# Attention scores on all 128 rows of the array, by padding with zeros, in a two-layer diffusion transformer step

## The chip, the cores and the metric

One core of a Trainium2 chip. The time is device microseconds (us) of one execution of the whole program. Before the change three runs gave 918.04, 919.28 and 920.19 us; the median is 919.28.

## The reference

One inference step of a hybrid backbone with two layers of width 1024. There are 128 prompt (context) tokens and 256 sample (latent) tokens that share all weights, and 128 cached keys and values. Each layer has a mixer (differential attention, a short gated convolution, a chunk MLP, all from one input projection and into one output projection) and a squared-ReLU MLP of hidden width 4096. What matters here is the attention, with 4 heads; a head's queries and keys have two components of 64 features each:

```
s = einsum('bqhcd,bkhcd->bchqk', q, k) * 64 ** -0.5    # c: the two components
p = softmax(s, axis=-1)
a = p[:, 0] - lam * p[:, 1]
o = einsum('bhqk,bkhd->bqhd', a, v)
```

Prompt queries read the 128 prompt keys. Sample queries read the 128 cached keys and the 256 sample keys (384 columns). Sample queries and keys take an axial rotation first (rotary positions). The result must be near fp32.

## The kernel before

Activations lie with features on partitions and tokens along the free dimension: `x` is 128 x 8 x 384. Weights stream from HBM in chunks of 128 x 1024 fp32 values. ScalarE rounds each chunk to a high part (`whi`, line 201), VectorE subtracts to get the low part (`wlo`, line 203), and TensorE multiplies three times per contraction step: high by high, high by low, low by high (lines 220 to 222). These long products fill nearly all of TensorE's time.

All engines run in an order written out at build time. `tick()` counts the contraction steps of the long products, and every side task is a generator that yields how many steps may pass before its next stage; the table `WAIT` holds these numbers. So the score products, transposes and value products stand at fixed places between the long products in TensorE's queue, and each of the other engines has its own fixed order too. Two further kinds of work are woven in: modulation products on TensorE (`pm`, line 262, which use 32 columns of the array) and modulation sums on VectorE (line 314).

Per head:

- `keys(h)` (line 653): the cached keys are loaded, the sample's keys are rotated (`rope_apply`: one shuffle on VectorE, three products and sums on GpSimd), and the sample's and cached keys are split. The high part `kh` holds each component on both halves of the partitions (lines 666 and 669). The low part `kl` holds component 0 on rows 0 to 63 and component 1 on rows 64 to 127 (line 670).
- `queries(h)` (line 672): the sample's queries are rotated and split into `qs`, per component a tile whose own half holds the high part (line 682) and whose other half holds the low part (line 685). With `kh` on both halves, one 128-row product gives high by high plus low by high.
- `attention(h, u)`: `u` = 0 is the prompt's block of queries, 1 and 2 are the sample's two blocks. The prompt's scores are plain fp32 products of 64 rows (line 728; an fp32 product shows as two instructions in the trace). The sample's are one 128-row product (line 731) and one 64-row product with the low key part (line 732), for each of the two components. Behind the scores come the maximum (VectorE, line 736), exponentials (ScalarE, 741), the combination of the two softmaxes (747 and 749), the transposes (TensorE, 753), their copies (ScalarE, 762 and 764), the value products (TensorE, 776), the head's norm and its transposes (797).

The first `NPRE` heads of a layer (3 and 2) have their products ahead of the norm. Their shift by the bias is added later, in `first_heads`, by ScalarE instructions over the prompt's and the sample's columns (lines 698 and 703). The other heads (1 and 2) come in `later_heads`; ScalarE drains their queries from PSUM in a single instruction over 384 columns (line 715). The shift itself needs small products of its own in layer 0 (lines 463 and 471, with a copy on ScalarE between them, line 467).

Of the kernel before, what the change touches and what calls it, by code (L numbers as in the profile page):

```python
# [9 lines left out]
F32 = mybir.dt.float32  # L10
F32R = mybir.dt.float32r
# [4 lines left out]
P = 128  # L16
# [3 lines left out]
TP = 128  # L20
TS = 256
T = TP + TS
# [5 lines left out]
# heads of a layer whose products go ahead of the norm  # L28
NPRE = (3, 2)
# parts of the first modulation vector  # L30
PARTS = 4

# contraction steps between the stages of the work beside the long products, by layer
# [53 lines left out]
# columns of the packed small operands: those of all layers that come first, then the rest  # L87
# [5 lines left out]
# order of the 128-column tiles of the input projection  # L93
Q0, K0, V0, GB0, GC0, XI0, U0, VS0 = 0, 512, 1024, 1536, 1792, 2048, 2304, 2560

# tokens, followed by one column for the shift of each group
# [4 lines left out]
def dit_kernel(ctx, tc, xT, cT, wmod, wmodT, wall, ck, cv, ws, lam, bs_in, small, rope, ident_in, yT, kT_out, v_out):  # L101
# [10 lines left out]
    # ---- constants and inputs  # L112
# [16 lines left out]
    # silu of the two conditioning vectors, as padded stationary columns  # L129
# [8 lines left out]
    # ---- the order of work: every engine runs in the order below. What is not part of the long  # L138
    # products is cut into stages; a stage names how many contraction steps of the long products
    # go by before the next one.  # L140
# [33 lines left out]
    def steps(gen, n, every):  # L174
        """n stages of a generator"""
        for i in range(n):
            next(gen, None)
            if i < n - 1:
                yield every

    # ---- weight streaming
# [8 lines left out]
    def refill(r=None):  # L190
        """the next chunk of the weights, in two parts"""
        i = state["chunk"]
        if i == wall.shape[0]:
            return
        state["chunk"] = i + 1
        if r is None:
            r = raw_chunk(wall[i])
        hi = wpool.tile([P, 1024], F32R, tag="whi", name="whi", bufs=4)
        lo = wpool.tile([P, 1024], F32R, tag="wlo", name="wlo", bufs=4)
        ready.append((hi, lo))  # L200
        nc.scalar.copy(hi, r)  # L201
        yield 2
        nc.vector.tensor_sub(lo, r, hi.bitcast(F32))  # L203
# [13 lines left out]
    def mm3(out, w, a, wsl, asl, first, last):  # L217
        """out += w.T @ a from the parts of both, w stationary"""
        (wh, wl), (ah, al) = w, a
        mm(out, wh[wsl], ah[asl], start=first, stop=False)  # L220
        mm(out, wh[wsl], al[asl], start=False, stop=False)  # L221
        mm(out, wl[wsl], ah[asl], start=False, stop=last)  # L222

    # ---- modulation vectors, features on partitions: modv[d][:, v, dt, group]
# [4 lines left out]
    def mod_done(d, v, base, dts=slice(0, KT)):  # L229
        """modv[d][:, v] = base + b_mod, and what scales the normed input"""  # L230

        def column(o):
            c = sm[:, d * S_LAYER + o + dts.start : d * S_LAYER + o + dts.stop]
            return c.unsqueeze(2).to_broadcast([P, dts.stop - dts.start, 2])

        nc.vector.tensor_add(modv[d][:, v, dts], base[:, dts], column(S_BMOD + v * KT))
        if v in (1, 4):
            nc.vector.scalar_tensor_tensor(
                (amix if v == 1 else amlp)[d][:, dts],
                modv[d][:, v, dts],  # L240
                1.0,
                column(S_NMIX if v == 1 else S_NMLP),
                ALU.add,
                ALU.mult,
            )

    def mod_products():
        """on the tensor engine: one feature tile of the contraction per step"""
        for i, (d, v) in enumerate(MOD_PE):
            pm = ps.tile([P, 256], F32, tag="mod", name="pm", bufs=1)  # L250
            tr = work.tile([P, KT, 32], F32, name="tr", tag="rtmp", bufs=1)
            # the first vector comes in parts of its features
            n = per = PARTS if i == 0 else 1
            width = 256 // n
            for f in range(n):
                own = slice(f * width, f * width + width)
                for q in range(KT // per):
                    w = ahead if (i, f, q) == (0, 0, 0) else raw_chunk(wmod[i, f * KT // per + q])
                    for k in range(per):
                        kt = q * per + k  # L260
                        for j in range(4):
                            mm(  # L262
                                pm[32 * j : 32 * j + 32, own],
                                sct[:, kt, :],
                                w[:, (4 * k + j) * width : (4 * k + j + 1) * width],
                                start=(kt == 0),
                                stop=(kt == KT - 1),
                            )
                    yield
                dts = slice(f * KT // n, (f + 1) * KT // n)  # L270
                nc.vector.transpose(tr[:, dts].rearrange("p a b -> p (a b)"), pm[:, own])
                mod_done(d, v, tr[:, :, 0:2], dts)
                yield
# [4 lines left out]
    # the two silu vectors along the free dimension, on every partition  # L278
# [4 lines left out]
    def spread_silu():  # L283
        """their high and low parts as rows, 32 features of each tile a row; then the sums of both parts"""
# [21 lines left out]
    def mod_sums():  # L306
        """on the vector engine: one group of one tile of the vector's features per step"""
# [16 lines left out]
    # ---- RMS statistics over the features (partitions)  # L324
# [13 lines left out]
    def rsqrt_refined(y, a, ms):  # L338
        """y ~ ms^-0.5 made exact by one Newton step"""
# [15 lines left out]
    def normed(scale, shift, every):  # L355
        """the normed and modulated input, a feature tile per stage"""
# [23 lines left out]
    def scaled_high(dt, scale):  # L380
        """a feature tile without its tokens' norms, which products take on afterwards"""
# [24 lines left out]
    def finish_x(dt, pacc, gate, scale, last=False):  # L406
        """the residual stream's tile after a product, and what the next norm needs of it"""
# [12 lines left out]
    def proj_tiles(a, n=1, cols=T, name="acc", order=tuple(range(KT)), later=0, make=acc_tile):  # L420
        """128-column tiles of a weight, transposed: [column, token]"""
# [11 lines left out]
    def proj_tokens(a, width):  # L433
        """`width` columns of a weight, tokens on partitions: three tiles [token, column]"""
# [21 lines left out]
    def shift_products(raws, bias, t0, t1):  # L456
        """what the shift adds to the columns of the raw tiles: [column, tile, group]"""
# [17 lines left out]
    # padded conv input: 0 | prompt | 0 | sample | 0  # L475
# [3 lines left out]
    KSEG = ((0, 0, TP, 0), (1, TP, T, 2 * TP))  # L479

# [3 lines left out]
    def lambdas(d):  # L484
# [10 lines left out]
        # -(e1 - e2 + li)  # L495
# [5 lines left out]
    for d in range(DEPTH):  # L501
# [5 lines left out]
        def evict(i):  # L507
            """a head's keys or queries but for the shift's part, which comes later"""
# [20 lines left out]
        # ------------------------------------------------ mixer  # L529
        # products with the tiles of two heads go ahead of the norm  # L530
# [122 lines left out]
        def keys(h):  # L653
            """positions, and the parts of the keys by component: the high ones on both halves, the low
            ones next to the queries' high ones"""
# [7 lines left out]
            kl = work.tile([P, T], F32R, name="kl")  # L663
# [4 lines left out]
            for c, (own, other) in enumerate(((LO, HI), (HI, LO))):  # L668
                nc.scalar.copy(kh[other, c], k[own, TP:])
                nc.vector.tensor_sub(kl[own], k[own, TP:], kh[own, c].bitcast(F32))  # L670

        def queries(h):
            """positions, and the parts of the sample's queries by component: high and low ones on the
            two halves, the high ones on the component's own"""
# [12 lines left out]
        def first_heads():  # L687
            for h in range(NPRE[d]):
# [12 lines left out]
                for g, s0, s1, off in KSEG:  # L701
                    qq = q_t[:, h, s0:s1]
                    nc.scalar.activation(qq, qq, AF.Identity, bias=bias[:, 2 * h + 1, g : g + 1])
# [4 lines left out]
        def later_heads():  # L708
            for h in range(NPRE[d], NH):
# [5 lines left out]
                nc.scalar.mul(q_t[:, h % 3], pq[:, 0:T], 0.125)  # L715
# [4 lines left out]
        def attention(h, u):  # L720
            """softmaxes of 128 queries of a head, combined and applied to the values"""
# [3 lines left out]
            for c in range(2):  # L725
                r = slice(64 * c, 64 * c + 64)
                if u == 0:
                    mm(sc[c][:, 0:TP], q_t[r, h % 3, 0:TP], k_t[r, h % 3, 0:TP], start=True, stop=True)
                else:
                    cols = slice((u - 1) * P, u * P)  # L730
                    mm(sc[c][:, 0:T], qs[:, c, cols], kh[:, c], start=True, stop=False)
                    mm(sc[c][:, 0:T], qs[r, c, cols], kl[r], start=False, stop=True)  # L732
# [45 lines left out]
            # norm of the head's output, tokens on partitions  # L778
# [45 lines left out]
        def conv(ct):  # L824
            """short convolution, channels on partitions"""
# [65 lines left out]
        # output projection  # L891
# [7 lines left out]
        # ------------------------------------------------ MLP  # L899
        if d == 1:  # L900
            start(steps(sums, 2 * KT, wt["sums_up"]), 2)
        for f in range(2):
# [33 lines left out]
            def down(pt, w, c, cols):  # L936
                """half of the contraction of a tile"""
# [13 lines left out]
    # ---- the last tiles, a group of tokens after the other, and the final norm of each group  # L951
# [40 lines left out]
# the vectors (layer, which) in the order of their use, by the engine that makes them  # L992
# [6 lines left out]
def _tiles(w, cols):  # L999
    """[1024, cols of one 128-tile] -> [128, 8 * 128]"""  # L1000
# [5 lines left out]
def _pack(inp):  # L1006
# [6 lines left out]
    # [d, k, (v dt j c)] -> [v, kt, p, (j dt c)] and [v, dt, p, k]  # L1013
    # the first vector: [part, some kt, p, (kt j dt c)]
# [52 lines left out]
    # axial rotary tables by shape: partition = (component, axis, half, frequency)  # L1067
# [34 lines left out]
```

## Time and profile before

| | |
|---|---|
| span of the profiled execution, first to last instruction | 916.9 us |
| its device time apart from the span | not listed; the three runs' median is 919.28 us |
| TensorE products busy | 894.1 us, 98% |
| TensorE weight loads busy (they lie beside products) | 839.8 us, 92% |
| VectorE / ScalarE / GpSimd busy | 652.9 / 478.5 / 81.3 us |
| mean granted TensorE clock | 0.993 |
| data transfers | all issued by SyncE; queue kinds "hardware_dynamic" and "instruction" |

Times are microseconds from the span's start unless marked ns. A row of the timeline gives the start, the duration, the engine, the line, the operation, what it writes and reads, the shape, and in brackets the idle time before it and what ended that. Products are pipelined, so a product's duration (0.34 us) is longer than the distance between the starts of two of them (0.17 us); what a product costs TensorE's order is read from the starts. `64*128` is the part of the array that a product uses, rows by columns. The attention of layer 0 lies between 60 and 180 us, that of layer 1 between 500 and 600 us.

### The profile page before, as it was taken

To read this page: it belongs to the slowest core of one execution; us is meant where nothing else is said; L and a number is where in the kernel's file an instruction comes from. 1 tells how busy PE (TensorE), PEld (TensorE's weight loads), DVE (VectorE), ACT (ScalarE), POOL (GpSimd) and SP (SyncE) were. 2 spreads that over 40 slices of the span, in tenths; PEclk is the share of its full clock that TensorE was granted. 3 is DMA by queue.
4 is the path that set the end of the run, shared out by engine and by line. 5 is a ranking of instruction groups with operands and counts; after the bars stand their busy time and mean duration, and the time that the engine had idled before them with its cause. 6 is when DMAs were issued, how large, how long until landed. Compare 5 with 4: busy or idle time off the path is not lost.

```text
span 916.9 us, 14490 instructions
## 1 busy us (share of the span) xinstructions
PE 894.1 (98%) x5476; PEld 839.8 (92%) x5476; DVE 652.9 (71%) x1214; ACT 478.5 (52%) x938; POOL 81.3 (9%) x79
## 2 busy tenths in 40 slices
PE   5999999999999999999999999999999999999996
PEld 4766787999999999999998788999999999999996
DVE  4688886789888877879979877458886344555333
ACT  4557765446762226663336786534676223665331
POOL 0004320011000000000112340003000000000021
PEclk9999999999999999999999899999999999999998
DMA  9877566455656765566773323224465434333302
GB/s 346 298 274 252 192 209 226 165 182 161 209 188 226 227 214 180 183 198 226 221 234 101 125 76 95 91 93 138 163 221 169 137 117 136 115 133 121 115 1 69
DMA packets 48470, 156.55 MB, mean 171 GB/s; under 512 B 5392, under 2 KB 11024, under 8 KB 48400
## 3 DMA queue, kind: packets, MB, share of 16 engines
q1 hardware_dynamic: 48400, 155.63, 51.4%
q8 instruction: 43, 0.70, 0.3%
q14 instruction: 27, 0.22, 0.1%
HBM read 152.98 MB, written 2.62 MB: 170 GB/s over the span
## 4 chain that ended last, share of the span: by engine, by line
PE 91%; DVE 5%; DMA 1%; issue 1%; ACT 1%; POOL 1%; SPq 0%; DVEq 0%; ACTq 0%
PE pdn L220 10%; PE pdn L222 10%; PE pdn L221 10%; PE pup L221 9%; PE pup L220 9%; PE pup L222 9%; PE po L220 2%; PE po L221 2%; PE po L222 2%; PE pm L262 2%; PE pkq L220 2%; PE pkq L221 2%; PE pkq L222 1%; PE po L776 1%; PE nat L448 1%; PE sc L732 1%
## 5 line engine op out<-in xcount | busy, mean ns | idle before, releaser
L201 ACT CAST whi<-raw 128x1024 fp32r<-128x1024 f32 x182 | 190.0, 1050 | 293.3 <-PE pdn L221 150.9
L203 DVE TENSOR_TENSOR wlo<-raw,whi 128x1024 fp32r<-128x1024 f32 x182 | 224.6, 1240 | 64.9 <-ACT whi L201 64.8
L220 PE MATMUL pdn<-ah,whi 128*128 128x384 f32 (+2 forms) x528 | 174.7, 331 | 0.0
L221 PE MATMUL pdn<-al,whi 128*128 128x384 f32 (+2 forms) x528 | 174.6, 331 | 0.0
L222 PE MATMUL pdn<-ah,wlo 128*128 128x384 f32 (+2 forms) x528 | 174.6, 331 | 0.0
L220 PE MATMUL pup<-hh,whi 128*128 128x386 f32 x512 | 174.1, 340 | 0.0
L221 PE MATMUL pup<-hl,whi 128*128 128x386 f32 x512 | 173.6, 339 | 0.3
L222 PE MATMUL pup<-hh,wlo 128*128 128x386 f32 x512 | 172.8, 337 | 0.0
L314 DVE SCALAR_TENSOR_TENSOR junk<-raw,cb 128x1024 bf16<-128x1024 f32 x112 | 136.7, 1220 | 0.4
L221 PEld LDWEIGHTS pdn<-al,whi 128*128 128x128 f32 x528 | 99.2, 188 | 0.0
L220 PEld LDWEIGHTS pdn<-ah,whi 128*128 128x128 f32 x528 | 99.2, 188 | 0.0
L222 PEld LDWEIGHTS pdn<-ah,wlo 128*128 128x128 f32 x528 | 99.2, 188 | 0.0
L221 PEld LDWEIGHTS pup<-hl,whi 128*128 128x128 f32 x512 | 96.9, 189 | 1.1 <-DVE hl L387 0.9
L220 PEld LDWEIGHTS pup<-hh,whi 128*128 128x128 f32 x512 | 96.4, 188 | 0.3
L222 PEld LDWEIGHTS pup<-hh,wlo 128*128 128x128 f32 x512 | 96.5, 188 | 0.0
L336 POOL TENSOR_TENSOR sacc<-sacc,sq 128x384 f32<-128x384 f32 x23 | 29.4, 1279 | 675.6 <-ACT sq L329 533.7
L917 ACT ACTIVATE relu<-relu,ub 128x128 f32<-128x128 f32 (+1 forms) x128 | 51.1, 446 | 17.4 <-DVE relu L914 17.4
L398 DVE SCALAR_TENSOR_TENSOR x<-pdn,modv,x 128x128 f32<-128x128 f32 (+1 forms) x62 | 23.0, 413 | 43.9 <-PE pdn L222 43.9
L921 DVE TENSOR_TENSOR al<-relu,ah 128x384 fp32r<-128x384 f32 x64 | 35.6, 556 | 15.0 <-ACT ah L919 14.8
L220 PE MATMUL po<-y,whi 128*128 128x384 f32 x128 | 43.0, 336 | 0.0
L222 PE MATMUL po<-y,wlo 128*128 128x384 f32 x128 | 42.8, 334 | 0.0
L221 PE MATMUL po<-y,whi 128*128 128x384 f32 x128 | 42.8, 334 | 0.0
(198 smaller groups left out, 1414.1 us busy)
## 6 DMA issues: line engine op xcount, KB each, us to landing
raw<-in_wall_dram SPq DMA_DIRECT2D x182, 512.0 KB, 3.6
raw<-in_wmodT_dram SPq DMA_DIRECT2D x56, 512.0 KB, 4.3
raw<-in_wmod_dram SPq DMA_DIRECT2D x40, 512.0 KB, 5.7
raws<-in_wall_dram SPq DMA_DIRECT2D x6, 512.0 KB, 8.0
x<-in_xT_dram SPq DMA_DIRECT2D x8, 192.0 KB, 7.8
out_dram<-x SPq DMA_DIRECT2D x4, 256.0 KB, 2.6
mix<-in_cv_dram SPq DMA_DIRECT2D x2, 256.0 KB, 5.7
mix<-in_ws_dram SPq DMA_DIRECT2D x2, 256.0 KB, 6.0
```

The costliest lines, as they stand in the source:

```text
L201: nc.scalar.copy(hi, r)
L203: nc.vector.tensor_sub(lo, r, hi.bitcast(F32))
L220: mm(out, wh[wsl], ah[asl], start=first, stop=False)
L221: mm(out, wh[wsl], al[asl], start=False, stop=False)
L222: mm(out, wl[wsl], ah[asl], start=False, stop=last)
L262: mm(pm[32 * j : 32 * j + 32, own], sct[:, kt, :], w[:, (4 * k + j) * width : (4 * k + j + 1) * width], start=(kt == 0), stop=(kt == KT - 1),)
L314: nc.vector.scalar_tensor_tensor(junk, w, 1.0, cb[:, g], ALU.mult, ALU.mult, accum_out=mr[:, dt, g : g + 1])
L336: eng.tensor_add(stat["acc"], stat["acc"], sq)
L398: nc.vector.scalar_tensor_tensor(x[:, dt, a:b], pacc[:, a:b], gate[:, dt, g : g + 1], x[:, dt, a:b], ALU.mult, ALU.add)
L448: mm(o, ah, wh[:, cols], start=(kt == 0 and tt % n == 0), stop=False)
L917: nc.scalar.activation(r[:, s0:s1], r[:, s0:s1], AF.Relu, bias=ub[:, g : g + 1])
L921: nc.vector.tensor_sub(al[:, i], r, ah[:, i].bitcast(F32))
```

## The change

The low part of the keys becomes two static tiles per component, of 128 rows, with zeros in the other component's rows: component 0's low keys on rows 0 to 63 of `kl[:, 0]`, component 1's on rows 64 to 127 of `kl[:, 1]`. They meet all 128 rows of `qs`; the rows with the queries' low parts meet zeros. The prompt's queries go into tiles `qp`, again one per component with zeros in the other's rows, and meet all 128 rows of the prompt's keys. The zeros are written once, by GpSimd at the start; the rest of the program writes only the other halves. ScalarE therefore writes the prompt's queries in two 64-row instructions and the sample's in another one. To make room in SBUF, the program is built with a smaller DMA scratch. Comments are removed as well, which the diff below leaves out.

```diff
+    kl_t = [const.tile([P, 2, T], F32R, name=f"kl{i}") for i in range(2)]
+    qp_t = [const.tile([P, 2, TP], F32, name=f"qp{i}") for i in range(3)]
+    for t in (*kl_t, *qp_t):
+        nc.gpsimd.memset(t.bitcast(F32), 0.0)
...
         def keys(h):
...
-            kl = work.tile([P, T], F32R, name="kl")
+            kl = kl_t[h % 2]
...
-                nc.vector.tensor_sub(kl[own], k[own, TP:], kh[own, c].bitcast(F32))
+                nc.vector.tensor_sub(kl[own, c], k[own, TP:], kh[own, c].bitcast(F32))
...
         def first_heads():
...
-                for g, s0, s1, off in KSEG:
-                    qq = q_t[:, h, s0:s1]
-                    nc.scalar.activation(qq, qq, AF.Identity, bias=bias[:, 2 * h + 1, g : g + 1])
+                qb = bias[:, 2 * h + 1]
+                for c, own in enumerate((LO, HI)):
+                    nc.scalar.activation(qp_t[h % 3][own, c], q_t[own, h, 0:TP], AF.Identity, bias=qb[own, 0:1])
+                nc.scalar.activation(q_t[:, h, TP:T], q_t[:, h, TP:T], AF.Identity, bias=qb[:, 1:2])
...
         def later_heads():
...
-                nc.scalar.mul(q_t[:, h % 3], pq[:, 0:T], 0.125)
+                for c, own in enumerate((LO, HI)):
+                    nc.scalar.mul(qp_t[h % 3][own, c], pq[own, 0:TP], 0.125)
+                nc.scalar.mul(q_t[:, h % 3, TP:T], pq[:, TP:T], 0.125)
...
         def attention(h, u):
...
-                r = slice(64 * c, 64 * c + 64)
                 if u == 0:
-                    mm(sc[c][:, 0:TP], q_t[r, h % 3, 0:TP], k_t[r, h % 3, 0:TP], start=True, stop=True)
+                    mm(sc[c][:, 0:TP], qp_t[h % 3][:, c], k_t[:, h % 3, 0:TP], start=True, stop=True)
                 else:
                     cols = slice((u - 1) * P, u * P)
                     mm(sc[c][:, 0:T], qs[:, c, cols], kh[:, c], start=True, stop=False)
-                    mm(sc[c][:, 0:T], qs[r, c, cols], kl[r], start=False, stop=True)
+                    mm(sc[c][:, 0:T], qs[:, c, cols], kl[:, c], start=False, stop=True)
...
-    nc = bacc.Bacc("TRN2", target_bir_lowering=False, num_devices=1)
+    nc = bacc.Bacc("TRN2", target_bir_lowering=False, num_devices=1, dynamic_dma_scratch_size=4096)
```

## Rows read from the trace of the kernel before

**Rows 1.** Page: TensorE's busy time and weight loads; the chain's shares by engine.

```profile
PE 894.1 (98%) x5476; PEld 839.8 (92%) x5476; DVE 652.9 (71%) x1214; ACT 478.5 (52%) x938; POOL 81.3 (9%) x79
...
PE 91%; DVE 5%; DMA 1%; issue 1%; ACT 1%; POOL 1%; SPq 0%; DVEq 0%; ACTq 0%
```

**Rows 2.** Stretches: start:end, length, busy us of each engine, clock, DMA share, GB/s.

```profile
60.00:180.00 120.00, 119.30 (x800) 92.74 (x800) 94.51 (x213) 72.32 (x188) 24.66 (x24) 1.00 0.64 214
99.80:112.40 12.60, 12.60 (x78) 9.58 (x76) 11.63 (x26) 9.18 (x27) 2.81 (x4) 1.00 0.56 183
502.00:512.00 10.00, 7.17 (x21) 4.88 (x20) 9.89 (x17) 7.02 (x14) 5.04 (x6) 0.66 0.25 81
514.00:530.00 16.00, 16.00 (x86) 13.65 (x85) 12.49 (x29) 13.10 (x32) 4.36 (x6) 1.00 0.40 138
```

**Rows 3.** Instructions of the score tile: count, duration ns (least/median/most), starts, shape.

```profile
L732 PE MATMUL sc<-kl,qs x32: 435/439/445, 79.9 to 580.6; 64*128 64x384 f32 x32
```

**Rows 4.** Timeline of TensorE around one sample block of layer 0.

```profile
87.67 0.34 PE L222 MATMUL pgc<-hh,wlo 128*128 128x384 f32 x1
87.85 0.34 PE L731 MATMUL sc<-kh,qs 128*128 128x384 f32 x1
88.12 0.44 PE L732 MATMUL sc<-kl,qs 64*128 64x384 f32 x1
88.49 0.44 PE L731 MATMUL sc<-kh,qs 128*128 128x384 f32 x1
88.86 0.44 PE L732 MATMUL sc<-kl,qs 64*128 64x384 f32 x1
89.23 0.44 PE L220 MATMUL pxi<-hh,whi 128*128 128x384 f32 x1
89.52 0.34 PE L221 MATMUL pxi<-hl,whi 128*128 128x384 f32 x1
```

**Rows 5.** Timeline of TensorE around one prompt block of layer 0.

```profile
94.46 0.34 PE L222 MATMUL pxi<-hh,wlo 128*128 128x384 f32 x1
94.73 0.49 PE L728 MATMUL sc<-mix 64*128 64x128 f32 x4
95.15 0.44 PE L220 MATMUL pgb<-hh,whi 128*128 128x384 f32 x1
95.43 0.34 PE L221 MATMUL pgb<-hl,whi 128*128 128x384 f32 x1
```

**Rows 6.** Timeline of TensorE around three full-array fp32 transposes.

```profile
91.79 0.34 PE L222 MATMUL pxi<-hh,wlo 128*128 128x384 f32 x1
91.96 0.49 PE L753 MATMUL pt<-ident,e 128*128 128x128 f32 x3
...
92.47 0.34 PE L221 MATMUL pxi<-hl,whi 128*128 128x384 f32 x1
```

**Rows 7.** TensorE's waits: line, what it waited for, us, times, longest.

```profile
PE psb L471 <- ACT shb L467: 0.6, 1, 0.6
```

**Rows 8.** Timelines of ScalarE and TensorE ahead of a value product in layer 0.

```profile
125.42 0.46 ACT L764 COPY ats<-pt 128x384 f32<-128x384 f32 x1
...
126.48 1.50 PE L776 MATMUL po<-mix,ats 128*128 128x128 f32 x12
```

**Rows 9.** The same in layer 1, with the drain of a later head's queries.

```profile
528.67 0.48 ACT L715 ACTIVATE mix<-pq 128x384 f32<-128x384 f32 x1
...
533.41 0.48 ACT L764 COPY ats<-pt 128x384 f32<-128x384 f32 x1
...
534.23 1.50 PE L776 MATMUL po<-mix,ats 128*128 128x128 f32 x12
```

**Rows 10.** Timelines of VectorE and TensorE around one transpose of layer 1.

```profile
546.86 0.62 DVE L749 SCALAR_TENSOR_TENSOR e<-e,s 128x384 f32<-128x384 f32 x1
...
547.84 0.49 PE L753 MATMUL pt<-ident,e 128*128 128x128 f32 x3
```

**Rows 11.** Timeline of GpSimd: its first rotary product.

```profile
65.95 0.93 POOL L649 TENSOR_TENSOR rt<-mix,rp 128x256 f32<-128x256 f32 x1 [64.55 <-ACT mix L698]
```

## The prediction

> **What bounds the kernel now.** I read the page's busy shares first, then the chain that ended last: TensorE is busy 894.1 of 916.9 us, and 91% of the chain is its own work [rows 1]. So a microsecond taken from TensorE is a microsecond of the end, as long as no other engine is late for it. The table by stretches says where that could happen: in the two attention stretches VectorE and ScalarE are far from idle, and in some windows one of them is nearly full (VectorE 11.63 of 12.60 us, ScalarE 13.10 of 16.00 us) [rows 2]. The change therefore needs two readings: what TensorE's order loses, and which result of another engine it then meets too early.
>
> **What the change takes from TensorE.** Listing the score products gives 32 of the 64-row products with the low key parts, two in each block of a head's 128 sample queries, so 16 blocks [rows 3]. The timeline of one block shows what they cost. An ordinary product starts 0.17 to 0.18 us after the one before it; in the block the starts lie 0.27, 0.37, 0.37, 0.37 and 0.29 us apart, the last two of them belonging to the projection's products behind it. From the block's first start to the second product behind it are 89.52 - 87.85 = 1.67 us [rows 4]. The distance is long on both sides of every 64-row product, not only while one runs. After the change all four are 128-row products of the same 384 columns. Their distance has two bounds: 0.37 us (nothing won) and 0.175 us. I take 0.175, because the nearest row is the block's own first product: 128 rows, the same tiles, starting 0.18 us after the projection's last one [rows 4]. Then 5 x 0.175 = 0.88 us stand for 1.67, and a block saves 0.79 us. Two of the 16 are followed by modulation products of another column shape, which may keep a long distance of their own; for these I count only three distances, 3 x (0.37 - 0.175) = 0.59. Sum: 14 x 0.79 + 2 x 0.59 = 12.2 us.
>
> The prompt's blocks (4 heads in 2 layers, 8 of them) hold four 64-row instructions that run in pairs, 0.97 us from the last projection product to the second one behind (94.46 to 95.43) [rows 5]. Padded they are four full fp32 instructions of 128 columns. The nearest rows are the transposes, same shape and type: three of them take 0.68 us over the same distance (91.79 to 92.47) [rows 6], and one more adds (1.50 - 0.49) / (12 - 3) = 0.11 us, from the merged groups of 12 and of 3 [rows 6, 8]. So 0.79 us, a gain of 0.18. Other bound: they keep the pairs' distance without the pairing, which from 94.73 to 95.15 gives 0.42 us for two pairs, so 0.42 us more for four singles. I take the gain; 8 x 0.18 = 1.4 us, and 0.2 more where the first one of layer 1 runs at the lower clock. TensorE's order loses 13.8 us in all.
>
> Against this stands the page "TensorEngine Tiling (Array Packing)" of the Trainium skill, section Performance Considerations: with a contraction of 64 rows, two tiles of the array work side by side. The trace does show the pairing [rows 5], and by that rule alone the prompt's blocks would lose 8 x 0.42 = 3.4 us.
>
> **What it adds elsewhere.** ScalarE writes the prompt's queries in two 64-row pieces, each into its own component's tile: one more instruction for each of 5 early heads, two more for each of 3 later heads, 11 in all. Bounds for one: 0, and 0.48 us, what the late heads' single 384-column drain takes [rows 9]; the pieces share that one's work, so I take 0.2 us per head, nearer to nothing. That also moves the sample's part, which the rotary step waits for, behind the prompt's. The new memsets (2 x 768 and 3 x 256 elements per partition) lie on GpSimd behind the first one; even at the 0.93 us of its 256-element product they are 9 x 0.93 = 8.4 us, and its next rotary product comes after 64.55 us of idleness [rows 11]. I cost them at nothing; without that cover, up to 8.4 us at the start. VectorE's subtractions for the low keys keep their number and size; the key tiles rotate by two as before. Every data transfer is issued by SyncE to a hardware queue, so I cost the smaller DMA scratch at nothing as well.
>
> **What is late next.** TensorE now arrives early, and I go through the places in its order where it takes another engine's result.
>
> (a) The shift product behind layer 0's first sample block already waits 0.6 us for a copy on ScalarE [rows 7], which is fed by work from VectorE. The gain of the two blocks ahead of it, 0.18 + 0.59 = 0.8 us, becomes a longer wait.
>
> (b) At 126.48 us TensorE multiplies probabilities with values; the copy that it needs ended at 125.42 + 0.46 = 125.88, 0.6 us before [rows 8]. Between (a) and there it gains four sample blocks and two prompt blocks: 4 x 0.79 + 2 x 0.18 = 3.5 us. The chain to that copy runs through VectorE, GpSimd's rotary and ScalarE, and VectorE has only 0.97 us to spare from 99.8 to 112.4 [rows 2]; the rest of its lead, from the blocks before 99.8, is at most 0.97 (0.79 + 0.18). So the copy comes 0.8 to 1.9 us earlier, less 0.2 for the split drain ahead of it; the wait is 3.5 - 0.6 - (0.8 to 1.9) + 0.2 = 1.2 to 2.3, and I take 1.8 us.
>
> (c) The same step in layer 1: copy ended 533.41 + 0.48 = 533.89, product at 534.23 [rows 9]. In that layer VectorE is full from 502 to 512 (9.89 of 10.00 us) [rows 2] while TensorE already stands 2.8 us, and ScalarE works 13.10 of the next 16 us; so that chain does not start earlier, and its drain is split too (0.2 us). TensorE's lead there is 0.4 + 0.79 + 0.79 + 0.18 + 0.79 = 2.9 us, the slack 0.3: the wait is 2.9 - 0.3 + 0.2 = 2.8 us.
>
> (d) The transpose at 547.84 follows VectorE's combination (546.86 + 0.62 = 547.48) by 0.36 us [rows 10]. One block, 0.79, lies before it, and a split drain in ScalarE's order: 0.79 + 0.2 - 0.36 = 0.6 us at most; I take 0.5, as ScalarE's order there partly hangs on that block itself.
>
> Behind (d) and behind (b) the leads are re-anchored on TensorE's own score products, and I see none that uses up its slack. Weights come from transfers and splits that TensorE's progress itself releases. Given back: 0.8 + 1.8 + 2.8 + 0.5 = 5.9 us. Net 13.8 - 5.9 = 7.9 us. The profiled span becomes 916.9 - 7.9 = 909.0 us; the median of the runs stands 2.4 us above that span (919.3), so I predict 911.4.
>
> **Rivals.**
> Nothing is given back: ScalarE and VectorE follow at the pace of TensorE. For it: ScalarE idles 40% of the first attention stretch [rows 2], and the waits of (b) and (c) are argued, not seen. Against: the slack of 0.3 and 0.6 us. 919.3 - 13.8 = 905.5 us. Chance 0.20.
>
> The new waits lower the clock. The stand of 2.8 us in 502 to 512 goes with a granted clock of 0.66 over that window, a mix of 2.4 and 1.2 GHz [rows 2], which is 10 x 0.34 = 3.4 us of lost clock; (b) and (c) are waits of that order. Against: in layer 0 the 0.6 us wait of (a) left the stretch at 1.00. One drop gives 914.8, two 918.2. Chance 0.12, mostly one.
>
> The padding does not do what it says: the distance of 0.37 us belongs to these tiles or to changing weights, and stays. For it: nothing in the trace shows a 128-row low product. Against: the block's first product. Sample blocks gain nothing, prompt blocks lose up to 3.4 us: 919.3 to 922.7. Chance 0.05. The Trainium skill's page "TensorE: Matmul & The Clock Gate" (Packing small matmuls, The mechanism) says that weight loads overlap running products only when their row groups differ, which would bring this about; the trace disagrees in ordinary products, as weight loads are busy 839.8 us beside 894.1 us of products of the same 128 rows [rows 1].
>
> Slower: ScalarE's drain sets the end. If its chain were late in every head, as in (c), TensorE's gain would all turn into waiting, and the 11 added instructions, at 0.2 to 0.48 us, would come on top: 919.3 + 2.2 to 5.3 = 921.5 to 924.6. It decides where the slack before the transposes is below 0.2 us; at (d), one of the tightest, it is 0.36. Chance 0.05.
>
> **How the numbers follow.** The forecast has 0.58. Its own range is 908 to 914.5, from 1.2 to 2.3 in (b) and a lead in (c) between fully kept and fully lost with some more loss. The range for 8 in 10 adds the case without give-back and the single clock drop: 904.5 to 916. A change of under 0.2% (1.8 us, about what a measurement of this kernel can tell) is 917.4 to 921.1. Faster: 0.58 + 0.20 + 0.10 = 0.88; the same: 0.05 (two drops, the padding without effect and hidden); slower: 0.07.
>
> **What would show it.** In the changed kernel's timeline the score block's five starts should lie 0.17 to 0.18 us apart, the prompt's four 0.11; TensorE's busy time should fall by more than its span, and its list of waits should gain the value products of both layers and the shift product at 0.6 + 0.8 us. I am wrong if the starts stay at 0.37, if the waits at (b) and (c) are absent (905 to 907), or if the waits appear at transposes of every head.

## The result and the profile after

The changed kernel took 911.43 us (median of 4 runs, 910.83 to 912.79) against 918.66 for the kernel before in the runs with it: a ratio of 0.9932, 95% interval 0.9917 to 0.9948. A second set of runs gave 910.87 against 918.19, 0.9921 (0.9909 to 0.9934). The profiled execution took 911.23 us; its span is 909.4 us, 7.5 below the 916.9 of the span before.

The page of the changed kernel, busy times and the chain's shares by engine; they answer to [rows 1]:

```profile
PE 881.9 (97%) x5476; PEld 841.0 (92%) x5476; DVE 651.5 (72%) x1214; ACT 480.9 (53%) x949; POOL 84.2 (9%) x84
...
PE 84%; DVE 7%; ACT 3%; POOL 2%; issue 2%; DMA 1%; SPq 0%; DVEq 0%; ACTq 0%; POOLq 0%
```

TensorE's busy time fell by 12.2 us, the span by only 7.5. The difference, 4.7 us, is idle time that wasn't there before, and the chain points at the engines behind it: TensorE's share went from 91% to 84%, those of VectorE, ScalarE and GpSimd rose.

The timeline of TensorE around the same sample block as [rows 4], and the prompt block of [rows 5] (line numbers behind the change are those of each kernel's own text, so line 731 became 740):

```profile
88.06 0.34 PE L740 MATMUL sc<-kh,qs 128*128 128x384 f32 x1
88.23 0.34 PE L741 MATMUL sc<-kl,qs 128*128 128x384 f32 x1
88.40 0.34 PE L740 MATMUL sc<-kh,qs 128*128 128x384 f32 x1
88.58 0.34 PE L741 MATMUL sc<-kl,qs 128*128 128x384 f32 x1
88.76 0.33 PE L220 MATMUL pxi<-hh,whi 128*128 128x384 f32 x1
88.93 0.34 PE L221 MATMUL pxi<-hl,whi 128*128 128x384 f32 x1
...
93.90 0.34 PE L222 MATMUL pxi<-hh,wlo 128*128 128x384 f32 x1
94.08 0.61 PE L737 MATMUL sc<-mix,qp 128*128 128x128 f32 x4
94.44 0.42 PE L220 MATMUL pgb<-hh,whi 128*128 128x384 f32 x1
94.70 0.33 PE L221 MATMUL pgb<-hl,whi 128*128 128x384 f32 x1
```

The five starts of the sample block lie 0.17 to 0.18 us apart, 0.87 us in sum where it was 1.67. The prompt block takes 0.80 us (93.90 to 94.70) where it took 0.97.

TensorE's waits; each row is the line, what it waited for, us, times, and the longest. `po` is the value product, `sc` the score product, `psb` the shift product, `pt` the transpose. The row of the shift product was there before, with 0.6 us [rows 7]; the other three are new:

```profile
PE po L785 <- ACT ats L773: 2.1, 2, 1.3
PE sc L740 <- ACT e L750: 1.8, 3, 0.8
...
PE psb L471 <- ACT shb L467: 1.2, 1, 1.2
...
PE pt L762 <- DVE e L758: 0.4, 1, 0.4
```

The stretches, to be read beside [rows 2] (busy us of TensorE, weight loads, VectorE, ScalarE, GpSimd, then the clock):

```profile
60.00:180.00 120.00, 117.07 (x822) 97.49 (x821) 97.56 (x219) 76.88 (x200) 25.48 (x24) 1.00 0.64 215
...
498.00:508.00 10.00, 7.20 (x27) 5.55 (x26) 9.88 (x17) 7.25 (x15) 5.66 (x6) 0.83 0.27 94
```

In the first attention stretch TensorE now stands idle for nearly 3 us where it stood 0.7. The stand in layer 1's first products is the same 2.8 us as before; the half clock behind it lasted for less of the window in this profile (0.83 against 0.66). That is not where most of the time came from: the kernel with 64-row products, below, has no half clock at all from 500 to 510 us in its profile (1.00), and that profile's span, 915.4 us, is only 1.5 below the span before. The granted clock also differs between runs of one kernel: its mean lies between 0.990 and 0.997 in the listed runs of the kernel before. And the time that a full clock saves there is in part lost again at the next meeting of TensorE and ScalarE, the first sample block of layer 1: of the eleven profiles with the rotation (all but the last two runs below), the three whose clock is 1.00 from 500 to 508 us wait 1.6 to 1.9 us there, six others with 0.91 over 500 to 520 us wait 0.4 to 0.7, and the two with 0.83 don't wait.

### The profile page after: what moved, and what is told of

It reads as the page before. It is cut to its first block, busy times and chain, and to the rows that moved or that the text cites. A ratio compares the mean times of both kernels' runs of the same rounds, so it can differ in the third digit from the quotient of the medians.

```text
span 909.4 us, 14510 instructions
## 1 busy us (share of the span) xinstructions
PE 881.9 (97%) x5476; PEld 841.0 (92%) x5476; DVE 651.5 (72%) x1214; ACT 480.9 (53%) x949; POOL 84.2 (9%) x84
## 4 chain that ended last, share of the span: by engine, by line
PE 84%; DVE 7%; ACT 3%; POOL 2%; issue 2%; DMA 1%; SPq 0%; DVEq 0%; ACTq 0%; POOLq 0%
PE pdn L222 10%; PE pdn L220 10%; PE pdn L221 10%; PE pup L221 10%; PE pup L220 9%; PE pup L222 9%; PE po L222 2%; PE po L220 2%; PE po L221 2%; PE pkq L220 2%; PE pm L262 2%; PE pkq L221 2%; PE pkq L222 1%; DVE wlo L203 1%; PE po L785 1%
```

## The experiments

Two theories stand against each other for the gain, and two for what was given back. For the gain: the change of array shape (theory), or something else that came with the change. For the loss: a chain through VectorE, the rotation on GpSimd, and ScalarE that doesn't follow TensorE (theory), or something on TensorE's side, the clock or PSUM.

**All of the change, but 64-row products.**

```diff
+                r = slice(64 * c, 64 * c + 64)
-                    mm(sc[c][:, 0:TP], qp_t[h % 3][:, c], k_t[:, h % 3, 0:TP], start=True, stop=True)
+                    mm(sc[c][:, 0:TP], qp_t[h % 3][r, c], k_t[r, h % 3, 0:TP], start=True, stop=True)
-                    mm(sc[c][:, 0:T], qs[:, c, cols], kl[:, c], start=False, stop=True)
+                    mm(sc[c][:, 0:T], qs[r, c, cols], kl[r, c], start=False, stop=True)
```

> Everything of the change is in (static zeroed tiles, memsets, smaller DMA scratch, queries drained in pieces), but each score product reads only its component's 64 rows, as before the change. Theory (the 64-row shape costs, the rest is nearly free): starts in a sample block 0.27, 0.37, 0.37, 0.37, 0.29 us apart as before, prompt pairs 7 ns apart, time 918.5 to 920.5 us. Rival (the gain came with the tiles' place, the scratch or the new order on ScalarE): about 911.

918.05 against 918.02 us, ratio 1.0000 (0.9988 to 1.0012). Its block of the same place, from TensorE's timeline:

```profile
86.60 0.34 PE L741 MATMUL sc<-kh,qs 128*128 128x384 f32 x1
86.87 0.44 PE L742 MATMUL sc<-kl,qs 64*128 64x384 f32 x1
87.23 0.44 PE L741 MATMUL sc<-kh,qs 128*128 128x384 f32 x1
87.61 0.44 PE L742 MATMUL sc<-kl,qs 64*128 64x384 f32 x1
87.97 0.45 PE L220 MATMUL pxi<-hh,whi 128*128 128x384 f32 x1
88.26 0.34 PE L221 MATMUL pxi<-hl,whi 128*128 128x384 f32 x1
```

With 64 rows the block is back at 1.66 us and the gain is gone. The memsets, the smaller scratch, the tiles and the split drain together cost and bring nothing that shows in the time while TensorE isn't early. Its list of waits does have a new row, at the first sample block of layer 1; it goes with this profile's full clock, as said above:

```profile
PE sc L741 <- ACT e L751: 1.6, 1, 1.6
```

**The low keys alone, and the prompt's queries alone.** The first keeps `kl_t` and drops `qp_t`, with ScalarE's drain as before the change; the second does the reverse.

```diff
 # low keys alone
...
-                    mm(sc[c][:, 0:TP], qp_t[h % 3][:, c], k_t[:, h % 3, 0:TP], start=True, stop=True)
+                    mm(sc[c][:, 0:TP], q_t[r, h % 3, 0:TP], k_t[r, h % 3, 0:TP], start=True, stop=True)
 # prompt alone
...
-                    mm(sc[c][:, 0:T], qs[:, c, cols], kl[:, c], start=False, stop=True)
+                    mm(sc[c][:, 0:T], qs[64 * c : 64 * c + 64, c, cols], kl[64 * c : 64 * c + 64], start=False, stop=True)
```

> Only the low keys are padded; the prompt's queries and their 64-row products stay. Theory: the sample blocks carry 12.2 of the 13.8 us that TensorE's order loses, starts 0.17 to 0.18 apart; some 5 us come back as waits, 911.5 to 913 us. Rival (nothing is given back without the split drain on ScalarE): 906.5.

> Only the prompt's queries are padded; low keys stay at 64 rows. Theory: 0.18 us per block, 1.4 to 1.6 us off TensorE's order, half of it lost at the shift product and in layer 1, and 0.2 us per head more on ScalarE: 917.3 to 919.3. Rival (pairs of 64-row products are worth keeping): 8 x 0.42 us more, 921 to 922.

Low keys alone: 909.37 us, ratio 0.9912 (0.9898 to 0.9925), which is 2 us better than expected. Prompt alone: 917.89 us, ratio 1.0007 (0.9994 to 1.0020), as expected. So the low keys carry the whole gain. That padding the prompt on top of them costs something (909.4 against 910.9 and 911.4) is likely but not shown: the intervals of the ratios overlap, and the two kernels did not share a chip. TensorE's waits with the low keys alone:

```profile
PE po L782 <- ACT ats L770: 1.7, 2, 0.9
...
PE psb L471 <- ACT shb L467: 1.2, 1, 1.2
...
PE sc L737 <- ACT e L747: 0.7, 2, 0.4
```

The wait at the shift product is the changed kernel's; those at the value and score products are shorter, and the one at the transpose is gone. The drain in one piece on ScalarE fits that (its price stands under (b) below); TensorE is also less early here, by the gain of the prompt's blocks, and this run doesn't tell the two apart.

**Nothing padded, the two 64-row products side by side.**

```diff
             for c in range(2):
...
                     mm(sc[c][:, 0:T], qs[:, c, cols], kh[:, c], start=True, stop=False)
-                    mm(sc[c][:, 0:T], qs[r, c, cols], kl[r], start=False, stop=True)
+            if u > 0:
+                for c in range(2):
+                    r = slice(64 * c, 64 * c + 64)
+                    mm(sc[c][:, 0:T], qs[r, c, cols], kl[r], start=False, stop=True)
```

> The kernel before, with the two 64-row low products of a sample block moved behind both 128-row ones, so that they lie side by side on the two halves of the array; nothing is padded. Theory (the cost hangs on going from 128 to 64 rows and back): starts 0.17, 0.27, 0.01, 0.37, 0.28 apart, 1.10 us where it was 1.67, some 9 us off TensorE's order, 3 to 4 of them lost to waits: 912.5 to 914.5. Rival (each 64-row product costs its 0.37 by itself): 917 to 919.

910.31 us, ratio 0.9915 (0.9902 to 0.9928), again better than expected. TensorE's timeline merges the pairs:

```profile
86.91 0.51 PE L731 MATMUL sc<-kh,qs 128*128 128x384 f32 x2
87.35 0.45 PE L735 MATMUL sc<-kl,qs 64*128 64x384 f32 x2
87.73 0.45 PE L220 MATMUL pxi<-hh,whi 128*128 128x384 f32 x1
88.01 0.34 PE L221 MATMUL pxi<-hl,whi 128*128 128x384 f32 x1
```

The block takes 1.10 us (86.91 to 88.01), and the two 64-row products, of which the merged row is no longer than one (0.45 us), run together. So two that run together pay once what each paid alone, for one excursion from 128 to 64 rows and back: 1.67 = 5 x 0.175 + 2 x 0.40 before, 1.10 = 4 x 0.175 + 1 x 0.40 here. Whether two 64-row products one behind the other would also pay once is not shown. A kernel without any padding gains as much as the change: it wins less on TensorE (1.67 - 1.10 = 0.57 us per block), but TensorE's list gains less too, 0.4 us more at the shift product and 0.4 at a value product:

```profile
PE psb L471 <- ACT shb L467: 1.0, 1, 1.0
...
PE po L779 <- ACT ats L767: 0.4, 1, 0.4
```

**GpSimd writes the padded prompt queries.** The cut shows the later heads; the early heads are changed in the same way.

```diff
...
-                for c, own in enumerate((LO, HI)):
-                    nc.scalar.mul(qp_t[h % 3][own, c], pq[own, 0:TP], 0.125)
-                nc.scalar.mul(q_t[:, h % 3, TP:T], pq[:, TP:T], 0.125)
+                nc.scalar.mul(q_t[:, h % 3], pq[:, 0:T], 0.125)
+                for c, own in enumerate((LO, HI)):
+                    nc.gpsimd.tensor_copy(qp_t[h % 3][own, c], q_t[own, h % 3, 0:TP])
```

> The changed kernel once more, beside its variants on one chip: 910.5 to 912 us.

> The changed kernel, but ScalarE drains the queries as before the change and GpSimd copies the prompt's halves into the padded tiles. Theory (the split drain on ScalarE delays the copies and transposes that TensorE waits for): the waits at the value products and at the transpose shrink by 0.2 to 0.5 us each, 909.5 to 910.5 us. Rival (the late chain is VectorE's and GpSimd's, and the copies make it later): 911.5 to 912.5.

912.68 us, ratio 0.9936 (0.9922 to 0.9950), beside 910.87 for the changed kernel on that chip: near the rival's numbers (each of the five runs is slower than each of the five of the changed kernel, though the intervals of the ratios overlap). The wait at the transpose went and those at the score products fell from 1.8 to 1.3 us, but those at the value products rose from 2.4 to 3.3. The copies stand ahead of the rotation in GpSimd's queue, 1.68 us for a later head's two in layer 0, and the value product of layer 0 became later. First its wait, then two stretches of that kernel around it (TensorE, weight loads, VectorE, ScalarE, GpSimd, clock):

```profile
PE po L787 <- ACT ats L775: 1.7, 1, 1.7
```

```profile
122.00:126.00 4.00, 2.25 (x20) 1.41 (x19) 1.39 (x6) 1.75 (x5) 2.09 (x3) 0.99 0.95 322
126.00:130.00 4.00, 4.00 (x17) 3.96 (x18) 3.93 (x10) 3.47 (x13) 0.00 (x0) 0.58 0.68 245
```

TensorE stood 1.7 us and then ran the next 4 us mostly at 1.2 GHz. In the two profiles of the changed kernel it stood 1.3 and 1.5 us at the same place and stayed at 2.4 GHz.

**The late value products 3 steps later.** In the changed kernel and in the one with low keys alone; in the changed one a transpose too.

```diff
-            yield wt["at4"]
+            yield wt["at4"] + (1 if (d, h, u) == (1, 1, 2) else 0)
...
-            yield wt["at6"]
+            yield wt["at6"] + {(0, 1): 3, (1, 0): 3}.get((d, h), 0)
```

> The changed kernel with the two late value products moved 3 contraction steps back in TensorE's order (layer 0 head 1, layer 1 head 0) and one transpose one step (layer 1 head 1). Theory (TensorE only meets these results too early): the waits of 1.3, 0.9 and 0.4 us go, 908.5 to 909.5 us. Rival (the chain behind them is the bound and the lateness moves on to the next place): 911 to 911.5.

> Only the low keys padded, and the two late value products 3 contraction steps later. Theory: 2 us of waits go from the kernel with padded keys alone, 907 to 908 us. Rival (lateness moves on): 909 to 909.5.

Both got slower: 913.43 us (0.9957, 0.9943 to 0.9970) and 913.32 us (0.9950, 0.9937 to 0.9962). My expectation was wrong, and the rival, which had the mechanism, put the time too low. The waits at the value products went, and longer ones came at the transposes of the head's norm behind them (`pot`); the waits of the retimed kernel and two of its stretches:

```profile
PE pot L806 <- DVE o L800: 4.4, 2, 3.2
...
PE sc L740 <- ACT e L750: 2.3, 2, 1.9
```

```profile
537.00:541.00 4.00, 1.05 (x6) 0.73 (x5) 3.65 (x10) 3.92 (x10) 2.08 (x3) 0.97 0.00 0
541.00:545.00 4.00, 3.79 (x15) 3.82 (x16) 2.10 (x5) 2.34 (x7) 0.06 (x1) 0.61 0.38 124
```

The 1.9 us at a score product are again those of the first sample block of layer 1, before which the clock had stayed at 1.00. A delay in this schedule moves the stage in all queues and every stage behind it. ScalarE's timeline of the second kernel shows what the norm's steps fell behind: the split of the next keys, which itself waits for a score product to release its tile. With the low keys alone the same norm step came first (531.86 us, the split at 534.74).

```profile
533.09 1.04 ACT L672 CAST kh<-mix 64x384 fp32r<-64x384 f32 x2 [0.51 <-PE sc L737]
534.14 0.28 ACT L788 ACTIVATE o<-po 128x128 f32<-128x128 f32 x1
```

**The late value products 2 steps later, with the norm held in its place.** On the kernel with low keys alone:

```diff
+            moved = 2 if (d, h) in ((0, 1), (1, 0)) else 0
-            yield wt["at6"]
+            yield wt["at6"] + moved
...
-            yield wt["at7"]
+            yield wt["at7"] - moved // 2
...
-            yield wt["at8"]
+            yield wt["at8"] - moved // 2
```

> Only the low keys padded; the two late value products 2 contraction steps later, but the norm steps behind them stay where they were in all queues. Theory (moving the whole tail of the head put its norm behind the next keys): 907.5 to 908.5 us, no wait at value products nor at the norm's transposes. Rival: lateness moves on again, 909 to 913.

908.51 us, ratio 0.9902 (0.9887 to 0.9917): the fastest of all kernels that compute the whole step and at the edge of what was expected, but not told apart from low keys alone (0.9912). The value products wait no more; 1.2 us at the norm's transposes stand there instead, so half of the expectation failed. This kernel differs from the one above in two things, 2 steps for 3 and the norm's place, and no run tells which of them mattered.

**Without the rotation.** The calls of `rope_apply` are taken out of the kernel before and of the changed one.

```diff
-            rope_apply(k[:, 2 * TP :])
...
-            rope_apply(q[:, TP:T])
```

> The kernel before without the rotation of queries and keys (the shuffle on VectorE and three steps on GpSimd per head and side are left out). All theories: 916 to 919 us, as these steps delay TensorE little there.

> The changed kernel without the rotation. Theory (what is given back comes from the chain through VectorE, the rotation on GpSimd and ScalarE, which doesn't get faster with TensorE): the waits at the value products go, and against the kernel before without rotation it is 11 to 13 us faster, not 7.5. Rival (TensorE's leads are eaten elsewhere, as by the clock or by PSUM): still 7 to 8 us.

911.90 us and 900.28 us (4 runs each, 911.27 to 912.59 and 899.78 to 900.48; same chip): the change is worth 11.6 us here (11.0 by the spans of the two profiles), against 7.2 and 7.3 with the rotation. The pages' busy rows, first without the change, then with it:

```profile
PE 890.8 (98%) x5476; PEld 838.3 (92%) x5476; DVE 634.3 (70%) x1182; ACT 477.8 (53%) x938; POOL 33.3 (4%) x31
```

```profile
PE 877.9 (98%) x5476; PEld 840.1 (94%) x5476; DVE 633.4 (71%) x1182; ACT 480.1 (53%) x949; POOL 35.2 (4%) x36
```

and the only wait on an attention result that is left in the second:

```profile
PE pt L760 <- DVE e L756: 0.3, 1, 0.3
```

TensorE's busy time falls by 12.9 us, and nearly all of it reaches the end. So what was given back came through the queues that carry the rotation. This kernel takes work from VectorE, GpSimd and their queues at once; which of the three matters most it doesn't tell. Both kernels of the pair have a clock of 1.00 from 500 to 510 us, so the pair alone doesn't set the clock aside; that the clock stayed at 1.00 behind the new waits of the changed kernel does, but for a small part (see the rivals below). My number for the kernel before without rotation was wrong: at 911.90 it is 5.3 us faster than the kernel before, where I had 916 to 919. Its stretch from 500 to 510 us shows most of the reason; there is no stand in layer 1's first products any more (2.8 us before), and no half clock:

```profile
500.00:510.00 10.00, 10.00 (x46) 7.51 (x45) 9.70 (x23) 9.36 (x22) 0.00 (x0) 1.00 0.52 160
```

## Why the prediction was right, point by point

**TensorE's order loses 13.8 us.** Right in the blocks shown: 0.80 us per sample block by the two timelines (0.79 forecast) and 0.17 per prompt block (0.18). One prompt block of layer 0, which modulation products follow, gained nothing (0.69 us from the projection's last product to them before, 0.71 after). The busy time, in which a product's overlap with the next is counted, fell by 12.2 us. That the low product with 128 rows would run like the block's first product was the choice that carried the forecast, and it held.

**The additions cost nothing by themselves.** Right in the time: ratio 1.0000 with 64-row products. The pieces on ScalarE matter only where TensorE is early; there I had 0.2 us for a drain in pieces, and it cost 0.46, as (b) shows.

**(a) 0.8 us at the shift product.** Nearly right in sum (1.0), split over two places: the wait there grew by 0.6 us, and 0.4 us more appeared at the score product ahead of it, one of the three `sc` waits.

**(b) 1.8 us at layer 0's value product.** 1.3 us measured, near the lower end of the 1.2 to 2.3 that I derived. But three terms of the sum were off, and that they nearly cancel is luck. Before the change, ScalarE's drain and GpSimd's first rotary product behind it:

```profile
119.50 0.49 ACT L715 ACTIVATE mix<-pq 128x384 f32<-128x384 f32 x1
...
120.13 0.74 POOL L649 TENSOR_TENSOR rt<-mix,rp 128x256 f32<-128x256 f32 x1 [4.75 <-ACT mix L715]
```

and after it, with the copy and the value products:

```profile
118.73 0.55 ACT L724 ACTIVATE qp<-pq 64x128 f32<-64x128 f32 x2
119.30 0.39 ACT L725 ACTIVATE mix<-pq 128x256 f32<-128x256 f32 x1
...
119.82 0.74 POOL L656 TENSOR_TENSOR rt<-mix,rp 128x256 f32<-128x256 f32 x1 [5.21 <-ACT mix L725]
...
125.10 0.46 ACT L773 COPY ats<-pt 128x384 f32<-128x384 f32 x1
...
123.48 0.83 PE L785 MATMUL po<-mix,ats 128*128 128x128 f32 x6
125.61 0.94 PE L785 MATMUL po<-mix,ats 128*128 128x128 f32 x6 [1.30 <-ACT ats L773]
```

The row at 126.48 [rows 8] merges twelve products. The copy that I held against it belongs to the sample's second block, and only the last six read it, 6 x 0.11 = 0.67 us later: the slack was 1.3 us, not 0.6. The drain began 0.77 us earlier than before, at the lower end of my 0.8 to 1.9, but the rotation behind it only 0.31 us earlier, so the pieces cost 0.46 us, not 0.2. And TensorE's lead at these products was 3.0 us (126.48 against 123.48), not 3.5. With these terms the wait is 3.0 - 1.3 - 0.77 + 0.46 = 1.4 us. With the drain in one piece, in the kernel with low keys alone, it is 0.9.

**(c) 2.8 us at layer 1's value product.** The mechanism was right, the place was too narrow. TensorE met the late chain in three places: the waits between 500 and 600 us are two at score products, 1.4 us together, and 0.8 at the value product, 2.2 in all (the transpose belongs to (d)).

```profile
PE sc L740 <- ACT e L750: 1.4, 2, 0.8
PE po L785 <- ACT ats L773: 0.8, 1, 0.8
PE pt L762 <- DVE e L758: 0.4, 1, 0.4
```

I had noted only when results are ready, not when a score tile's place in PSUM becomes free: a score product waits there until ScalarE has taken the exponentials of an earlier one. The slack was misread as in (b), 1.0 us instead of 0.3, as here too only the last six of the twelve products read the late copy. And 0.6 us of the 2.2, at the first sample block, is not the change's alone: with only the prompt padded the same place waits 0.5 us at the same clock.

**(d) 0.5 us at the transpose.** 0.4 measured.

**The sum.** New waits: 0.6 + 2.1 + 1.8 + 0.4 = 4.9 us against 5.9 forecast; span 7.5 us shorter against 7.9. The two accounts differ in what they count: a wait's row begins when the last product has ended, some 0.17 us after the next one could have started. By starts, as the forecast was made, and with its 13.8 us, 13.8 - 7.5 = 6.3 us came back. That 911.4 was met so closely is partly luck: the two sets of runs of the changed kernel differ by 0.6 us, and two errors cancel in it. The span is 909.4, not 909.0 us, and the runs stand 1.7 to 1.9 us above their spans, not 2.4.

**The rivals.** Nothing given back (905.5): refuted here, but it is nearly what happens without the rotation. The clock falling in the new waits: it did not happen in the changed kernel, but it does in variants whose waits are longer (1.7 and 3.2 us), so the chance of 0.12 was not too much. A small part of what came back may still be the clock: 14 of 39 listed runs of the kernel before have a mean clock of 0.997, and none of the nine of the changed kernel (0.993 to 0.995). Padding without effect, and weight loads that can't overlap within the same rows: refuted by starts 0.17 apart. ScalarE's drain setting the end: refuted. One rival I did not have: that half of the cost could be saved in a different way, by order alone.

## What to carry to other kernels

Look at the distance between starts on both sides of a product whose shape differs from its neighbours': here a change of shape had a price on each side, and putting the small products side by side may win as much as padding them, without new work for other engines. On an engine that is 98% busy, follow every microsecond you free to the next result that this engine takes from another; here more than a third of it came back as waits, and slack of less than the lead is the place to look. Read that slack at the first product that needs the late result, not at the start of a merged row. Moving a late consumer in a schedule with one count of steps for all queues moves its followers too, so see where these land; that holding them in place was the cure here is not shown.

## What the runs showed that I had not expected

One excursion to 64 rows and back costs 0.40 us beside 384-column products, whether one product stands in it or two that run side by side. Two 64-row products of 384 columns on different halves of the array take the time of one. A stand of TensorE of 1.7 us was followed by a stretch at a mean granted clock of 0.58; stands of 1.3 and 1.5 us at the same place were not. The length of the stand alone doesn't decide it: the 2.8 us in layer 1 went with a half clock in the profiles of the kernel before and of the changed one, and with none in that of the kernel with 64-row products. Where there was none, a wait of 1.6 us at the first sample block stood in its place, so clock that is saved at one stand need not all reach the end.
